# A two-layer encoder trunk: the Hyena filter stored in both parts, its constants and the first products of layer 1 placed anew

## Chip, core and metric

One NeuronCore of a Trainium2 chip runs the whole program. The metric is device time in microseconds (us) of one execution; lower is better.

## What is computed

`x` is 512 tokens by 1024 channels, float32. Layer 0 mixes tokens by latent attention and neighbourhood attention, layer 1 by retention and by a long convolution (Hyena); after each comes a gated feed-forward network with 2816 inner channels. The part that the change is about, cut down:

```python
def hyena_operator(u_proj, short_conv, ..., hy_bias):
    x0, x1, v = jnp.split(dwconv3(u_proj, short_conv), 3, axis=-1)
    h_f, h_b = hyena_filters(L, ...)
    k_circ = jnp.concatenate([h_f, zeros, h_b[1:][::-1]], axis=0)
    u = v * x1
    uf = jnp.fft.rfft(u, n=2 * L, axis=1)
    kf = jnp.fft.rfft(k_circ, n=2 * L, axis=0)
    y = jnp.fft.irfft(uf * kf[None], n=2 * L, axis=1)[:, :L]
    return (y + u * hy_bias) * x0
def bidirectional_retention(rq, rk, rv, rg, decay_fwd, decay_bwd):
    log_f = jax.nn.log_sigmoid(decay_fwd)
    ...
    return rms(o_f + o_b) * jax.nn.silu(rg)
```

## The kernel before

Channels lie on the 128 partitions, tokens in the free dimension. Every float32 matrix is split in two parts, `hi` (rounded to float32r) and `lo` (the remainder), and a product is three matmuls: hi·hi, lo·hi, hi·lo (`mm`, L280 to L282). Weights come in pieces of 128x1024 (`load_weight`, L250): SP loads `raw` (two buffers), ACT casts it to `whi`, DVE subtracts to get `wlo`; there are four buffers of each part, and weights are asked for three ahead. A projection of 128 output channels is 24 matmuls over eight tiles of `h` (`gemm`).

PSUM has eight banks by tag: `pj` two, `A` three, `B` two, `C` one. A product with a tag must wait until an older bank of that tag has been emptied.

A layer's normalization ends in `boundary` (L339). It updates `x`, writes the new `h`, starts the first four projections of the next stage without the token factor (`pre`), and then computes the factor itself: sums of squares by PE (`stats`, L286), the power -1/2 by POOL (`rcol`, L299), four transposes by PE into a `C` bank (`spread`, L316), and ACT's copy to `Rb` (L447). Projections are multiplied by `Rb` when they leave PSUM.

The filter of the long convolution is computed in layer 0's feed-forward stage (`filters`, L963) and stored to DRAM (`filt`) as float32. In layer 1 (`mixer1`, L1061) `dft_consts` loads the transform's constants `dftf` by two DMAs of POOL; `spectrum` (L1008) is a generator: for each of four pairs of parity and trig it loads two tiles `sd` of the filter by ACT's queue, splits them and makes two products `psC` of six matmuls. `mixer1` spills `x` to DRAM (L1065), convolves twelve projections (`conv`, L1072: `v`, then `x1`, then `x0`) with a step of `spectrum` after each of the last eight, transposes `u` (L1101), transforms (`dft`), multiplies spectra on DVE (`pq`, L1140), projects retention's `rv` (`proj_tok`), three `gate`s (L1106), and then makes the inverse transform with `dfti`, four groups of 24 matmuls in `A` banks. `decays` (L1040) computes 8 log decays in 26 small operations of DVE and one of ACT.

A scheduler sets the order on each engine from data dependences, buffer releases and priorities (`high_priority`); `issue_after` keeps an instruction behind a given one. Each engine then runs its queue strictly in order. Lines such as L282 are those of the kernel before; in the queues of the changed kernel shown further down they are that kernel's own, three to a hundred further on.

Of the kernel before, what the change touches and what calls it, by code (L numbers as in the profile page):

```python
# [16 lines left out]
P = 128  # L17
# [188 lines left out]
class Body:  # L206
    def __init__(self, ctx, tc, I, out, dbg=None):
        self.tc, self.nc, self.I, self.out, self.dbg = tc, tc.nc, I, out, dbg
        nc = self.nc
        pool = lambda n, b, **k: ctx.enter_context(tc.tile_pool(name=n, bufs=b, **k))  # L210
        self.cp = pool("cp", 1)
        self.wp = pool("wp", 4)
        self.xp = pool("xp", 8)
        self.hp = pool("hp", 16)
        self.sp = pool("sp", 6)
        self.pp = pool("pp", 8, space=bass.MemoryType.PSUM)
        self.dp = pool("dp", 1, space=bass.MemoryType.DRAM)
# [32 lines left out]
    def load_weight(self, n=1):  # L250
# [88 lines left out]
    def boundary(self, pool, tag, x, prod, gpost, gpre, ns, ftag, perm=False, rin=None):  # L339
# [529 lines left out]
    def ffn(self, p, x, h, pre, l):  # L869
# [18 lines left out]
        for j in range(FT):  # L888
# [5 lines left out]
            nc.vector.tensor_tensor(t, gps, Rb, ALU.mult)  # L894
# [35 lines left out]
    def dft_consts(self, p, name):  # L930
        out = []
        for i, part in enumerate(("hi", "lo")):
            t = p.tile([P, 4, 2, 256], F32R, tag="dft" + part, name=name + part)
            self.nc.gpsimd.dma_start(t.rearrange("p m a b -> p (m a b)"), self.I[name][:, i * 2048:(i + 1) * 2048])
# [28 lines left out]
    def filters(self, new):  # L963
# [28 lines left out]
        for tk in range(4):  # L992
# [10 lines left out]
            for i, src in enumerate((t, n)):  # L1003
                nc.sync.dma_start(self.filt[i, ts], src)
# [3 lines left out]
    def spectrum(self, mats, at, kt, spec):  # L1008
        nc = self.nc
        for par in range(2):  # L1010
            for trig in range(2):
                m = 2 * par + trig
                sd = []
                for hh in range(2):
                    t = self.X("sd", tag="xb")
                    tk = 2 * par + hh
# [3 lines left out]
                for ft in range(2):  # L1020
                    ps = self.PS("C")
                    for hh in range(2):
                        c = slice(ft * P, ft * P + P)
                        self.mm(ps, (mats[0][:, m, hh, c], mats[1][:, m, hh, c]), sd[hh], hh == 0, hh == 1)
                    if par == 0:
                        t = self.X("sp", tag="xb")
                        nc.scalar.activation(t, ps, AF.Copy, scale=1.0 / 512)
                        spec[ft, trig] = t
                    else:
                        e, o, d = spec[ft, trig], kt(), kt()  # L1030
                        nc.vector.scalar_tensor_tensor(o, ps, 1.0 / 512, e, ALU.mult, ALU.add)
                        if trig == 0:
                            nc.vector.scalar_tensor_tensor(d, ps, -1.0 / 512, e, ALU.mult, ALU.add)
                        else:
                            nc.vector.scalar_tensor_tensor(d, ps, 1.0 / 512, e, ALU.mult, ALU.subtract)
                        spec[ft, trig] = (o, d)
                    yield
# [23 lines left out]
    def mixer1(self, p, x, h, pre):  # L1061
        nc = self.nc
        spill = self.dp.tile([D, S], F32, name="xspill")
        for k in range(KT):
            nc.scalar.dma_start(spill[k * P:(k + 1) * P], x[k])  # L1065
        mats = self.dft_consts(p, "dftf")
# [5 lines left out]
        def conv(jj, dst):  # L1072
            ps = pre[jj - 8] if jj >= 8 else self.proj(h, "A" if jj == 4 else "pj")
            t = p.tile([P, S], F32, tag="cv", name=self.nm("cv"))
            nc.vector.tensor_tensor(t, ps, Rb, ALU.mult)
            cw = [self.col(C_SC + i * 12 + jj) for i in range(3)]
            nc.scalar.activation(dst, t, AF.Copy, scale=cw[1])
# [7 lines left out]
        u, x0 = [], [p.tile([P, S], F32, name=f"x0{j}") for j in range(4)]  # L1085
        for j in range(4):
            u.append(conv(8 + j, p.tile([P, S], F32, name=f"u{j}")))
# [84 lines left out]
        lg = self.decays(p)  # L1172
# [124 lines left out]
```

## Time and profile before

| | |
|---|---|
| timed runs | 1308.06, 1312.72, 1312.88 us; median 1312.72 |
| profiled execution | 1307.53 us, its span 1305.8 us |
| busy in the span | PE 97%, weight load 81%, DVE 62%, ACT 45%, POOL 6% |
| granted TensorE clock, mean | 0.993 of full |
| chain that ended last | PE 87%, DVE 5%, ACT 3% |
| retention and Hyena of layer 1 | 668 to 905 us of the span |

The span runs from the first to the last instruction. PE does nearly all that decides the time; what the other engines do matters where PE waits for it. The list of PE's waits and the timelines around them show these places.

### The profile page before, as it was taken

The page shows a single profiled execution, that of the slowest core. Times are in us where ns is not written, and L with a number is a line of the kernel's source. Part 1 is how long each engine was busy: PE and PEld are TensorE (multiplying, and loading weights), DVE is VectorE, ACT ScalarE, POOL GpSimd, SP SyncE. Part 2 cuts the span into 40 slices and gives each one's busy share as a digit, 9 for nine tenths or more (in the row PEclk, how much of TensorE's full clock was granted, in tenths as well). Part 3 has the DMA queues.
Part 4 walks back from the last instruction along what each step waited for, and adds up shares of the span by engine and source line. Part 5 has one row for each costly group of instructions (what it writes and reads, how often), then busy time and mean ns, then how long its engine had stood idle before and what let it go on. Part 6 is the DMA issues. An engine that isn't in the chain of part 4 may idle for free.

```text
span 1305.8 us, 16380 instructions
## 1 busy us (share of the span) xinstructions
PE 1271.7 (97%) x6370; PEld 1057.5 (81%) x6370; DVE 813.9 (62%) x1298; ACT 582.9 (45%) x943; POOL 80.9 (6%) x73
## 2 busy tenths in 40 slices
PE   9999799999999999999999999999999999999997
PEld 7788677997888788888987878778988888888886
DVE  6679898478766665322588785774875555552223
ACT  5456798456533333222454245544653333332221
POOL 4021322000000000000000000000000000000002
PEclk9999899999999999999999989999999999999999
DMA  7222012223434333333264233214233333333331
GB/s 269 86 65 79 3 33 68 82 79 116 121 123 135 122 113 97 99 111 97 83 226 128 58 120 95 81 49 130 66 113 98 97 97 97 97 97 104 107 97 65
DMA packets 41563, 130.62 MB, mean 100 GB/s; under 512 B 4652, under 2 KB 6892, under 8 KB 40973
## 3 DMA queue, kind: packets, MB, share of 16 engines
q1 hardware_dynamic: 35868, 116.92, 29.0%
q10 hardware_dynamic: 5040, 8.45, 2.0%
q0 software_dynamic: 576, 4.19, 0.9%
q8 instruction: 50, 0.82, 0.3%
q14 instruction: 29, 0.23, 0.1%
HBM read 123.26 MB, written 6.29 MB: 99 GB/s over the span
## 4 chain that ended last, share of the span: by engine, by line
PE 87%; DVE 5%; ACT 3%; issue 2%; DMA 1%; POOL 1%; SPq 0%; DVEq 0%; POOLq 0%; ACTq 0%
PE pspj L280 17%; PE pspj L282 17%; PE pspj L281 17%; PE psA L280 10%; PE psA L282 10%; PE psA L281 10%; DVE wlo L260 1%; ACT e L794 1%; DMA raw<-in_w 1%; PE psB L292 1%; PE psB L671 1%; PE psB L810 1%; DVE h L334 1%; ACT whi L259 1%; PE psC L282 1%
## 5 line engine op out<-in xcount | busy, mean ns | idle before, releaser
L259 ACT CAST whi<-raw 128x1024 fp32r<-128x1024 f32 (+1 forms) x200 | 209.1, 1048 | 432.1 <-PE pspj L281 237.8
L260 DVE TENSOR_TENSOR wlo<-raw,whi 128x1024 fp32r<-128x1024 f32 (+1 forms) x200 | 246.6, 1235 | 204.8 <-ACT whi L259 202.8
L280 PE MATMUL pspj<-h,whi 128*128 128x512 f32 (+1 forms) x664 | 250.5, 377 | 2.8 <-DVE v L599 2.7
L281 PE MATMUL pspj<-h,whi 128*128 128x512 f32 (+1 forms) x664 | 249.6, 376 | 0.0
L282 PE MATMUL pspj<-h,wlo 128*128 128x512 f32 (+1 forms) x664 | 249.4, 376 | 0.0
L282 PE MATMUL psA<-h,wlo 128*128 128x512 f32 (+1 forms) x424 | 155.4, 367 | 0.7 <-DVE wlo L260 0.7
L280 PE MATMUL psA<-h,whi 128*128 128x512 f32 (+1 forms) x424 | 156.1, 368 | 0.0
L281 PE MATMUL psA<-h,whi 128*128 128x512 f32 (+1 forms) x424 | 155.1, 366 | 0.0
L280 PEld LDWEIGHTS pspj<-h,whi 128*128 128x128 f32 x664 | 125.5, 189 | 25.4 <-DVE v L599 3.1
L282 PEld LDWEIGHTS pspj<-h,wlo 128*128 128x128 f32 x664 | 125.4, 189 | 22.2
L281 PEld LDWEIGHTS pspj<-h,whi 128*128 128x128 f32 x664 | 125.5, 189 | 22.0
L280 PE MATMUL pspj<-ahi,whi 128*128 128x512 f32 x308 | 121.4, 394 | 0.0
L282 PE MATMUL pspj<-ahi,wlo 128*128 128x512 f32 x308 | 120.7, 392 | 0.0
L281 PE MATMUL pspj<-alo,whi 128*128 128x512 f32 x308 | 119.5, 388 | 0.0
L282 PEld LDWEIGHTS psA<-h,wlo 128*128 128x128 f32 x424 | 79.8, 189 | 15.5 <-DVE wlo L260 1.9
L280 PEld LDWEIGHTS psA<-h,whi 128*128 128x128 f32 x424 | 80.0, 189 | 14.8 <-issue 2.6
L281 PEld LDWEIGHTS psA<-h,whi 128*128 128x128 f32 x424 | 80.0, 189 | 12.4
L894 DVE TENSOR_TENSOR t<-psA,Rb 128x512 f32<-128x512 f32 x40 | 27.6, 691 | 83.4 <-PE psA L282 83.3
L282 PEld LDWEIGHTS pspj<-ahi,wlo 128*128 128x128 f32 x308 | 57.8, 188 | 13.5
L281 PEld LDWEIGHTS pspj<-alo,whi 128*128 128x128 f32 x308 | 57.8, 188 | 12.9
L280 PEld LDWEIGHTS pspj<-ahi,whi 128*128 128x128 f32 x308 | 57.9, 188 | 11.5
L299 POOL TENSOR_TENSOR r<-v,mhalf 128x2 f32<-128x2 f32 (+1 forms) x14 | 13.7, 977 | 847.7 <-DVE v L297 690.2
(360 smaller groups left out, 2140.1 us busy)
## 6 DMA issues: line engine op xcount, KB each, us to landing
raw<-in_w SPq DMA_DIRECT2D x198, 512.0 KB, 3.5
x<-in_xT SPq DMA_DIRECT2D x16, 256.0 KB, 4.8
fflt<-in_fwin SPq DMA_DIRECT2D x8, 256.0 KB, 2.9
xspill<-f ACTq DMA_DIRECT2D x8, 256.0 KB, 2.6
sd<-filt ACTq DMA_DIRECT2D x8, 256.0 KB, 3.3
x<-xspill ACTq DMA_DIRECT2D x8, 256.0 KB, 3.2
rpb<-in_rpb SPq DMA_DIRECT2D x4, 384.0 KB, 4.6
filt<-fs SPq DMA_DIRECT2D x4, 256.0 KB, 2.5
```

What stands on the lines that cost most here:

```text
L259: nc.scalar.copy(hi[:, c], raw[:, c])
L260: nc.vector.tensor_tensor(lo[:, c], raw[:, c], hi[:, c].bitcast(F32), ALU.subtract)
L280: nc.tensor.matmul(ps, stat[0], mov[0], start=start, stop=False)
L281: nc.tensor.matmul(ps, stat[0], mov[1], start=False, stop=False)
L282: self.last_mm = nc.tensor.matmul(ps, stat[1], mov[0], start=False, stop=stop).ins
L292: nc.tensor.matmul(ps[:, j:j + 1], a[:, j * P:(j + 1) * P], self.ones, start=a is accs[0], stop=a is accs[-1])
L299: self.pow = nc.gpsimd.tensor_tensor(r, v, self.mhalf[:, :c], ALU.pow)
L334: self.nc.vector.scalar_tensor_tensor(lo, src, g, hi.bitcast(F32), ALU.mult, ALU.subtract)
L671: tr = lambda o, i: nc.tensor.transpose(o, i, self.ident)
L794: nc.scalar.activation(e, ps, AF.Exp, bias=nmx, accum_out=den[:, i:i + 1])
L810: nc.tensor.transpose(pt[:, i * P:(i + 1) * P], es[i][:, j * P:(j + 1) * P], self.ident)
L894: nc.vector.tensor_tensor(t, gps, Rb, ALU.mult)
```

## The change

**What it does.** `filt` holds both parts of the filter: after each step of `filters` ACT and DVE split the two results and SP stores four tiles instead of two. In layer 1, POOL loads the 16 stored tiles straight into the operands of `spectrum`, right behind the two constants `dftf`, all at high priority; the loads by ACT's queue and the eight splits are gone. The first four projections (`pre`) are scaled into `x0` tiles at once, all four, and convolved from there. The spill of `x` is issued behind the second `u`. `decays` is computed in layer 0's feed-forward stage. A `gate` and `rv` leave PSUM by an ACT copy, and DVE works on the copy in SBUF. A weight's cast by ACT is kept behind the last `Rb` copy (`hold`) if the weight is asked for after it.

```diff
-        self.filt = self.dp.tile([2, S, HC], F32, name="filt")
+        self.filt = self.dp.tile([2, 2, S, HC], F32, name="filt")
+        self.hold = None
...
             with self.tc.high_priority(WP):
-                nc.scalar.copy(hi[:, c], raw[:, c])
+                with self.tc.issue_after(self.hold) if self.hold is not None else ExitStack():
+                    nc.scalar.copy(hi[:, c], raw[:, c])
...
-            nc.scalar.copy(self.Rb, self.spread(self.rcol, "C"))
+            self.hold = nc.scalar.copy(self.Rb, self.spread(self.rcol, "C")).ins
...
-            nc.vector.tensor_tensor(t, gps, Rb, ALU.mult)
+            scaled = nc.vector.tensor_tensor(t, gps, Rb, ALU.mult)
+            if l == 0 and j == 4:
+                with self.tc.issue_after(scaled.ins):
+                    self.decay = self.decays(self.cp)
...
             for i, src in enumerate((t, n)):
-                nc.sync.dma_start(self.filt[i, ts], src)
+                hl = self.X("fh", F32R), self.X("fl", F32R)
+                self.split_to(*hl, src)
+                for part in range(2):
+                    nc.sync.dma_start(self.filt[part, i, ts], hl[part].bitcast(F32))
...
     def spectrum(self, mats, at, kt, spec):
+        for m in range(4):
+            parts.append([at(m % 2) for _ in range(2)])
+            for hh in range(2):
+                tk = 2 * (m // 2) + hh
+                for part in range(2):
+                    with self.tc.high_priority(300), self.tc.issue_after(self.consts):
+                        nc.gpsimd.dma_start(parts[m][hh][part], self.filt[part, m % 2, tk * P:(tk + 1) * P])
+        yield
...
-                    nc.scalar.dma_start(t, self.filt[trig, tk * P:(tk + 1) * P])
-                    sd.append(at(trig))
-                    self.split_to(*sd[-1], t)
...
     def mixer1(self, p, x, h, pre):
-        for k in range(KT):
-            nc.scalar.dma_start(spill[k * P:(k + 1) * P], x[k])
-        mats = self.dft_consts(p, "dftf")
+        x0 = [p.tile([P, S], F32, name=f"x0{j}") for j in range(4)]
+        with self.tc.high_priority(300):
+            mats = self.dft_consts(p, "dftf")
...
+        next(steps)
+
         for j in range(4):
-            u.append(conv(8 + j, p.tile([P, S], F32, name=f"u{j}")))
+            scaled(pre[j], x0[j])
+        u = []
+        for j in range(4):
+            u.append(conv(8 + j, p.tile([P, S], F32, name=f"u{j}"), x0[j]))
+            if j == 1:
+                with self.tc.issue_after(self.taken):
+                    for k in range(KT):
+                        nc.scalar.dma_start(spill[k * P:(k + 1) * P], x[k])
...
         def gate():
-            g, ps = self.X("rg", tag="xb"), self.proj(h)
-            nc.vector.tensor_tensor(g, ps, Rb, ALU.mult)
+            g = self.X("rg", tag="xb")
+            nc.scalar.copy(g, self.proj(h))
+            nc.vector.tensor_tensor(g, g, Rb, ALU.mult)
...
+            t = self.X("rv", tag="xb")
+            nc.scalar.activation(t, ps, AF.Copy, scale=rcol[:, j:j + 1])
             rv.append(two("t1"))
-            self.scaled(rv[-1], ps, rcol[:, j:j + 1], slice(0, S))
+            self.split_to(*rv[-1], t)
...
-        lg = self.decays(p)
+        lg = self.decay
```

**What it moves.** The programs' queues differ only here and in small exchanges in retention. First POOL's queue at the start of layer 1, before and now (`r` and `rcol` are the powers of the boundary, `filt` the stored filter; in brackets the semaphores waited for: DMASW are eight counters that POOL's transfers take in turn).

```order
L299 TENSOR_TENSOR r_5695<-v_5693,mhalf 128x2 [waits DVE_49]
L934 DMA dftfhi<-in_dftf 128x2048 [waits DMAHW2_49,DMAHW1_49,DMAHW5_49,DVE_49,DMAHW6_49,PE_49,Activation_49]
L299 TENSOR_TENSOR rcol_5879<-v_5982,mhalf 128x4 [waits DVE_49]
L934 DMA dftflo<-in_dftf 128x2048 [waits DMAHW6_49]
```

The same stretch of POOL's queue in the changed kernel:

```order
L302 TENSOR_TENSOR r_5767<-v_5765,mhalf 128x2 [waits DVE_49]
L940 DMA dftfhi<-in_dftf 128x2048 [waits PE_49,Activation_49]
L940 DMA dftflo<-in_dftf 128x2048 [waits PE_49]
L1026 DMA t_1107_6076<-filt 128x512 [waits DMAHW5_49]
...
L1026 DMA t_1110_6079<-filt 128x512 [waits DMAHW0_49,DMASW0_49]
...
L1026 DMA t_1118_6095<-filt 128x512 [waits DMAHW4_49,DMASW0_49]
L1026 DMA t_1122_6103<-filt 128x512 [waits DMAHW6_49,DMASW1_49]
L302 TENSOR_TENSOR rcol_5951<-v_6054,mhalf 128x4 [waits DVE_49]
L940 DMA dftihi<-in_dfti 128x2048 [waits DMASW2_49,PE_49]
```

The constants stood around `rcol`, the first behind a product of PE that belongs to the sum of squares. Now both constants and all 16 filter loads stand ahead of `rcol`, and from the seventh filter load on each waits for the transfer eight places before it.

PE's queue at the same place, before and now (`psA` is the fifth projection, `ident,rcol` the transposes for `Rb`, `psC<-t` the first product of the filter, `pspj` the sixth projection).

```order
L282 MATMUL psA_6036<-h_5592,wlo_5713 128x512
L316 MATMUL psC_5985<-ident,rcol_5879 128x128 [waits Pool_49]
L280 MATMUL psA_6036<-h_5594,whi_5712 128x512
...
L282 MATMUL psA_6036<-h_5600,wlo_5713 128x512
L280 MATMUL psC_6085<-t_1101_6075,dftfhi 128x512 [waits DMASW0_49,Activation_49]
L281 MATMUL psC_6085<-t_1102_6076,dftfhi 128x512 [waits DVE_49]
L280 MATMUL pspj_6094<-h_5586,whi_5718 128x512 [waits DVE_49]
L282 MATMUL psC_6085<-t_1101_6075,dftflo 128x512 [waits DMASW1_49]
```

The same place in the changed kernel:

```order
L285 MATMUL psA_6136<-h_5672,wlo_5785 128x512
L319 MATMUL psC_6057<-ident,rcol_5951 128x128 [waits Pool_49]
L283 MATMUL psC_6173<-t_1107_6076,dftfhi 128x512 [waits DMASW2_49,DMASW0_49,Activation_49]
L284 MATMUL psC_6173<-t_1108_6077,dftfhi 128x512 [waits DMASW4_49]
L285 MATMUL psC_6173<-t_1107_6076,dftflo 128x512 [waits DMASW1_49]
...
L284 MATMUL psC_6173<-t_1110_6079,dftfhi 128x512 [waits DMASW0_49]
L285 MATMUL psC_6173<-t_1109_6078,dftflo 128x512
L283 MATMUL pspj_6182<-h_5658,whi_5790 128x512 [waits DVE_49]
```

The transposes moved behind twelve more matmuls of the fifth projection and now stand directly ahead of the filter's product, which uses the same single `psC` bank; the wait for the constants is no longer spread over two places.

PE's queue at the inverse transform, before and now (the first row ends `proj_tok`; `pspj` are gates, `dfti` the inverse transform).

```order
L282 MATMUL psA_6659<-whi_6661,h_5601 128x512
L280 MATMUL psA_6898<-dftihi,t_1206_6550 128x256 [waits DMASW2_49,Activation_49]
L281 MATMUL psA_6898<-dftilo,t_1206_6550 128x256 [waits DMASW3_49]
L282 MATMUL psA_6898<-dftihi,t_1207_6551 128x256 [waits DVE_49]
...
L280 MATMUL psA_6898<-dftihi,t_1241_6648 128x256 [waits Activation_49]
L281 MATMUL psA_6898<-dftilo,t_1241_6648 128x256
L280 MATMUL pspj_6797<-h_5586,whi_6691 128x512 [waits DVE_49]
```

In the changed kernel `proj_tok` is followed by:

```order
L285 MATMUL psA_6711<-whi_6713,h_5673 128x512
L283 MATMUL pspj_6857<-h_5658,whi_6743 128x512 [waits Activation_49]
...
L285 MATMUL pspj_6892<-h_5672,wlo_6774 128x512
L283 MATMUL pspj_6927<-h_5658,whi_6803 128x512 [waits Activation_49]
...
L285 MATMUL pspj_6927<-h_5672,wlo_6804 128x512
L283 MATMUL psA_6961<-dftihi,t_1210_6602 128x256 [waits DMASW2_49]
L284 MATMUL psA_6961<-dftilo,t_1210_6602 128x256 [waits DMASW3_49]
L285 MATMUL psA_6961<-dftihi,t_1211_6603 128x256
```

The first group of the inverse transform stood ahead of the three gates, with a wait for nearly every operand; now it stands behind the gates' 72 matmuls, with the other three groups after it, and the gates wait for ACT where they waited for DVE.

## Rows read from the trace of the kernel before

**Rows 1.** The page's part 1, busy time by engine.
```profile
PE 1271.7 (97%) x6370; PEld 1057.5 (81%) x6370; DVE 813.9 (62%) x1298; ACT 582.9 (45%) x943; POOL 80.9 (6%) x73
```

**Rows 2.** Timeline of PE, layer 1's start: start, us, engine, line, op, [wait].
```profile
669.73 0.48 PE L280 MATMUL psA<-h,whi 128*128 128x512 f32 x1
...
672.98 0.65 PE L316 MATMUL psC<-ident,rcol 128*128 128x128 f32 x4
...
676.01 0.39 PE L282 MATMUL psA<-h,wlo 128*128 128x512 f32 x1
676.93 0.47 PE L280 MATMUL psC<-t,dftfhi 128*128 128x512 f32 x1 [0.53 <-DMA dftfhi<-in_dftf]
677.23 0.39 PE L281 MATMUL psC<-t,dftfhi 128*128 128x512 f32 x1
677.46 0.40 PE L280 MATMUL pspj<-h,whi 128*128 128x512 f32 x1
680.10 0.50 PE L282 MATMUL psC<-t,dftflo 128*128 128x512 f32 x1 [2.24 <-DMA dftflo<-in_dftf]
```

**Rows 3.** Timeline of POOL, 640 to 760 us.
```profile
645.50 1.08 POOL L299 TENSOR_TENSOR r<-v,mhalf 128x2 f32<-128x2 f32 x1 [8.04 <-DVE v L297]
...
671.52 1.40 POOL L299 TENSOR_TENSOR rcol<-v,mhalf 128x4 f32<-128x4 f32 x1 [0.28 <-DVE v L295]
672.89 0.59 POOL L934 DMA_DIRECT2D dftflo<-in_dftf  x1
...
748.52 0.54 POOL L934 DMA_DIRECT2D dftilo<-in_dfti  x1
```

**Rows 4.** Timeline of PE, fourth filter product and first transpose.
```profile
695.73 0.50 PE L280 MATMUL psC<-t,dftfhi 128*128 128x512 f32 x1 [0.69 <-ACT sp L1027]
...
698.64 0.50 PE L1101 MATMUL psB<-ident,u 128*128 128x128 f32 x2 [1.26 <-DVE u L1090]
```

**Rows 5.** Timeline of PE, inverse transform and the gate after it.
```profile
769.45 0.38 PE L280 MATMUL psA<-dftihi,t 128*128 128x256 f32 x1 [1.78 <-ACT t L274]
...
770.61 0.39 PE L282 MATMUL psA<-dftihi,t 128*128 128x256 f32 x1 [0.65 <-DVE t L275]
770.83 0.28 PE L280 MATMUL psA<-dftihi,t 128*128 128x256 f32 x1
770.95 0.28 PE L281 MATMUL psA<-dftilo,t 128*128 128x256 f32 x1
771.81 0.58 PE L282 MATMUL psA<-dftihi,t 128*128 128x256 f32 x1 [0.58 <-DVE t L275]
...
774.54 0.63 PE L280 MATMUL pspj<-h,whi 128*128 128x512 f32 x1
774.97 0.63 PE L281 MATMUL pspj<-h,whi 128*128 128x512 f32 x1
```

**Rows 6.** Stretches: us, busy PE, PEld, DVE, ACT, POOL, clock, DMA, GB/s.
```profile
742.00:766.00 24.00, 24.00 (x108) 19.86 (x107) 23.16 (x38) 7.18 (x10) 1.06 (x2) 1.00 0.32 110
...
772.00:778.00 6.00, 6.00 (x21) 5.23 (x22) 5.87 (x8) 3.06 (x5) 0.00 (x0) 0.50 0.36 96
```

**Rows 7.** DMA issues: queue, op, count, KB, median us to landing.
```profile
dftilo<-in_dfti POOLq DMA_DIRECT2D x1, 1024.0 KB, 7.4
```

**Rows 8.** Timeline of ACT, third weight's cast and the copy of the factor.
```profile
673.82 1.05 ACT L259 CAST whi<-raw 128x1024 fp32r<-128x1024 f32 x1 [0.80 <-DMA raw<-in_w]
674.78 0.57 ACT L447 COPY Rb<-psC 128x512 f32<-128x512 f32 x1
```

**Rows 9.** Tile `raw` (weights as loaded), 640 to 700 us, ten loads.
```profile
DMA to landing us min/median/max: 3.4/3.7/6.8
```

**Rows 10.** Timeline of DVE: a weight remainder, a multiply-add, a scaling.
```profile
687.44 1.23 DVE L260 TENSOR_TENSOR wlo<-raw,whi 128x1024 fp32r<-128x1024 f32 x1 [0.65 <-ACT whi L259]
688.58 0.74 DVE L1078 SCALAR_TENSOR_TENSOR u<-cv,cols,u 128x511 f32<-128x511 f32 x1
...
690.15 0.69 DVE L1075 TENSOR_TENSOR cv<-psA,Rb 128x512 f32<-128x512 f32 x1
```

More of the change, by code (lines that the diff above doesn't have):

```diff
@@ L933, in dft_consts @@
             t = p.tile([P, 4, 2, 256], F32R, tag="dft" + part, name=name + part)
-            self.nc.gpsimd.dma_start(t.rearrange("p m a b -> p (m a b)"), self.I[name][:, i * 2048:(i + 1) * 2048])
+            self.consts = self.nc.gpsimd.dma_start(t.rearrange("p m a b -> p (m a b)"), self.I[name][:, i * 2048:(i + 1) * 2048]).ins
             out.append(t)
@@ L1009, in spectrum @@
         nc = self.nc
[L1010 to L1013, printed above, removed]
-                for hh in range(2):
-                    t = self.X("sd", tag="xb")
-                    tk = 2 * par + hh
-                    nc.scalar.dma_start(t, self.filt[trig, tk * P:(tk + 1) * P])
-                    sd.append(at(trig))
-                    self.split_to(*sd[-1], t)
[L1020 to L1028, printed above, removed]
-                    else:
[L1030 to L1037, printed above, removed]
@@ new lines, in spectrum @@
+        parts = []
+        for m in range(4):
[6 more added lines that the diff above has]
+        yield
+        for m in range(4):
+            par, trig = m // 2, m % 2
+            sd = parts[m]
+            for ft in range(2):
+                ps = self.PS("C")
+                for hh in range(2):
+                    c = slice(ft * P, ft * P + P)
+                    self.mm(ps, (mats[0][:, m, hh, c], mats[1][:, m, hh, c]), sd[hh], hh == 0, hh == 1)
+                if par == 0:
+                    t = self.X("sp", tag="xb")
+                    nc.scalar.activation(t, ps, AF.Copy, scale=1.0 / 512)
+                    spec[ft, trig] = t
+                else:
+                    e, o, d = spec[ft, trig], kt(), kt()
+                    nc.vector.scalar_tensor_tensor(o, ps, 1.0 / 512, e, ALU.mult, ALU.add)
+                    if trig == 0:
+                        nc.vector.scalar_tensor_tensor(d, ps, -1.0 / 512, e, ALU.mult, ALU.add)
+                    else:
+                        nc.vector.scalar_tensor_tensor(d, ps, 1.0 / 512, e, ALU.mult, ALU.subtract)
+                    spec[ft, trig] = (o, d)
+                yield
@@ L1063, in mixer1, with scaled, conv @@
         spill = self.dp.tile([D, S], F32, name="xspill")
-        for k in range(KT):
-            nc.scalar.dma_start(spill[k * P:(k + 1) * P], x[k])
-        mats = self.dft_consts(p, "dftf")
+        x0 = [p.tile([P, S], F32, name=f"x0{j}") for j in range(4)]
+        with self.tc.high_priority(300):
+            mats = self.dft_consts(p, "dftf")
         two = lambda tag: tuple(p.tile([P, S], F32R, tag=tag, bufs=8, name=self.nm(tag)) for _ in range(2))
         rcol, Rb = self.rcol, self.Rb
-        def conv(jj, dst):
-            ps = pre[jj - 8] if jj >= 8 else self.proj(h, "A" if jj == 4 else "pj")
-            t = p.tile([P, S], F32, tag="cv", name=self.nm("cv"))
+        def scaled(ps, t):
             nc.vector.tensor_tensor(t, ps, Rb, ALU.mult)
+            return t
+        def conv(jj, dst, t=None):
+            if t is None:
+                t = scaled(self.proj(h, "A" if jj == 4 else "pj"), p.tile([P, S], F32, tag="cv", name=self.nm("cv")))
             cw = [self.col(C_SC + i * 12 + jj) for i in range(3)]
-            nc.scalar.activation(dst, t, AF.Copy, scale=cw[1])
+            self.taken = nc.scalar.activation(dst, t, AF.Copy, scale=cw[1]).ins
             nc.vector.scalar_tensor_tensor(dst[:, 1:], t[:, :S - 1], cw[0], dst[:, 1:], ALU.mult, ALU.add)
@@ L1084, in mixer1 @@
                               lambda: p.tile([P, S], F32, tag="t2", bufs=8, name=self.nm("ks")), ks)
-        u, x0 = [], [p.tile([P, S], F32, name=f"x0{j}") for j in range(4)]
+        next(steps)
         for j in range(4):
-            u.append(conv(8 + j, p.tile([P, S], F32, name=f"u{j}")))
+            scaled(pre[j], x0[j])
[6 more added lines that the diff above has]
+                        nc.scalar.dma_start(spill[k * P:(k + 1) * P], x[k])
         for j in range(4):
```

## Prediction, made before the changed kernel was run

> **What bounds the kernel now.** I read the page first: TensorE (PE) is busy in 97% of the span, so only the time in which PE stands still, or runs below full clock, can be won [rows 1]. The list of PE's waits came next: between 640 and 780 us, the start of layer 1, lie seven of them, and the feed-forward stages before and after hold almost none. Then PE's instructions in order of time at these places, where the reader should look at start times: at full clock one 512-column product starts 0.23 us after the last, as 677.46 after 677.23 [rows 2].
>
> Three stalls and one slow stretch matter:
> - *The front.* The first filter product waits 0.53 us for `dftfhi`, the third 2.24 us for `dftflo` [rows 2]: POOL issues `dftflo` only after it has computed `rcol` [rows 3].
> - *The fourth filter product and the first transpose* wait 0.69 us for ScalarE's (ACT's) copy out of the only `psC` bank, and 1.26 us for VectorE's (DVE's) first `u` times `x1` [rows 4].
> - *The inverse transform* waits 1.78, 0.65 and 0.58 us for `pq` values [rows 5]. DVE is the engine that is late there: it is busy 23.16 of 24 us [rows 6].
> - *The clock.* After those three gaps the granted clock of 772 to 778 us is 0.50, the lower of the two levels (1.2 GHz) [rows 6]; products start 0.43 us apart [rows 5].
>
> **What each part of the change is worth.** The sum is made against the profiled execution, 1307.53 us (span 1305.8 and 1.7 around it). The three timed runs have a median of 1312.72, 0.4% above it; I carry the gain in us over to that median.
>
> 1. *Constants and filter earlier: the 2.8 us of the front go.* The constants now lie over memory that the last feed-forward products free, and POOL reaches them once it has finished the second `r`, which ended at 646.6 [rows 3]. The first filter product needs them near 676. The filter's 16 quarter-MB transfers follow on POOL. An issue by POOL took 0.54 us [rows 3], so 18 take 10 us, to 657; this is the nearest row, as POOL has never issued this shape. The data: `dftilo`, the second of two MB issued one behind the other, landed 7.4 us after its issue, so the two came at some 265 GB/s [rows 3, 7]. Four MB are all that the last issue waits for (eight counters take turns, so the 18th waits for the 10th): 16 us, to 663. All six MB: 24 us, to 670. `rcol`'s power stands behind them on POOL and starts at 671.5 today; its transposes moved behind 12 more products (2.8 us), so it may start up to 2.8 us later, less hand-offs, at no cost. So this hides, with some 8 us to spare.
> 2. *What takes the front's place: 0.9 us.* The transposes of `rcol` and the first filter product now follow each other directly in the same `psC` bank; 12 products stood between them. ACT must copy the bank out first: 0.57 us [rows 8] and two hand-offs of some 0.16 us, the part of the 0.92 us between 676.01 and 676.93 that is neither wait nor pitch [rows 2]. Lower end 0.6. Upper end: the same copy stands behind the cast of the third weight, which was ready at 674.87, 0.8 us before the transposes would end (24 x 0.23 after 669.73, plus 0.4 for the four transposes, whose 0.65 us overlap with what follows: 675.65) [rows 2, 8]. Its load took the usual 3.4 us; the slowest took 6.8 [rows 9]. If it is slowed that much by the filter's transfers the wait grows by 2.6, to 3.5 us.
> 3. *First products: 1.3 us go.* DVE first empties the four banks, then convolves. Ahead of the first `u` times `x1` it has 5 scalings, 10 shifted multiply-adds and 3 weight remainders, at 0.60, 0.66 and 1.14 us from start to start (rows of 0.69, 0.74 and 1.23, which overlap by 0.09) [rows 10]: 13 us; from 676.4 that is 689.4, and up to 690.6 with waits for ACT. PE gets to the transposes after 66 products from 676.4: 691.6. The spare time is the 26 small operations of `decays` and the eight splits of `sd`, which left this place. ACT's eight spill issues move in between `u1` and `u2`, some 3.3 us; they are covered by DVE's work on `u0` and `u1`.
> 4. *The `psC` copy: 0.1 goes.* Two filter products still follow each other with only two transposes between. I keep 0.6 of the 0.69 us.
> 5. *Products between the transforms leave by ACT, and the inverse transform moves behind three gates: 3.0 us and the slow clock go.* The last `pq` that it waited for came before 771.81 [rows 5], and PE now comes there after 72 products, 16.5 us later. The gates need two `pspj` banks. Before, DVE freed them, behind all its `pq` work; now ACT does, as soon as the products end, and ACT has room (7.18 of 24 us) [rows 6]. The clock: 12 products of 256 columns took 2.73 us (771.81 to 774.54) and would take 1.44 at a pitch of 0.12; eight more lost 0.20 each. That is 1.3 + 1.6 = 2.9 us [rows 5].
> 6. *At nothing:* eight more casts on ACT, eight subtractions on DVE, eight stores on SP and the `decays` with one more table load, all in the first feed-forward stage, where PE is not kept waiting and weights lie three ahead (16 us of products). If that cover went, each of the four filter steps could cost a store's landing, for which a tile of the next block now waits: at most the 7.4 us of the slowest row [rows 7]. The weight casts behind `Rb` keep the copy of part 2 from standing behind two more casts; alone they win nothing.
>
> Each removed gap also takes a restart of about 0.16 us with it, six gaps, 1.0 us. Sum: 2.8 + 1.3 + 0.1 + 3.0 + 2.9 + 1.0 - 0.9 = **10.2 us**. The profiled execution would be 1297.3, the median **1302.5 us**, 0.8% faster. With the ends of part 2, the gain lies between 7.6 and 10.5.
>
> **Rivals.**
> - *POOL becomes the bound; slower.* `rcol`, and with it every product's scale, is behind 18 issues. At p us per issue POOL is free at 646.6 + 18p; from about 673.8 on, each us is lost. p = 1.5 costs nothing, p = 2.1 eats the gain, p = 2.5 is 0.5% slower. At 2.7, five times the row, POOL is free at 695.2, 21.4 us are lost, 11.2 net: 1324. For it: DVE is busy almost without pause in that stretch too, and the shape is new on POOL. Against it: the issue at 748.52 took 0.54 us [rows 3] within a stretch in which DVE was 97% busy [rows 6]. The Trainium skill, SBUF — State Buffer, "SBUF: two separate sides", speaks against this change: descriptors of POOL's transfers are written through a port that DVE locks in some modes, and a transfer of 0.62 us alone took 3.1 there; by that figure the kernel would come out near 1331 (an estimate). But it names copies, casts and `tensor_scalar` for this, and `tensor_tensor` not, and the row at 748.52 agrees with that. Chance 0.06.
> - *The front's wait comes back in another form; no change.* The third weight comes 3.4 us late (2.6 more at the copy), the first `u` stays late (1.3), and its late banks cost a us: gain 5.3, 1307.4. For it: ACT's and DVE's queues are in order, with 3.3 us of new issues in ACT's. Against it: the transfers should be over when that weight is asked for, at 670.2. Chance 0.20.
> - *The move doesn't do what it says at the inverse transform:* ACT's copy of the first gate stands behind casts that wait for DVE's `pq`; if a gate then waits as long as the transform did, the clock falls as well and 6.4 us stay: gain 3.8, 1308.9. Against it: those `pq` were there by 771.81 [rows 5], and that bank is wanted again only 48 products, 11 us, after the transform's old start. Chance 0.10.
>
> **How the numbers follow.** Forecast 0.64 (gains of 7.6 to 10.5 and a little beyond), rivals 0.06, 0.20 and 0.10. About 0.5% (6.6 us) is what a measurement of this kernel can tell from no change; the runs before lie between 1308.06 and 1312.88. Faster by more than that: the forecast and a third of the two middle rivals, where only half of their loss comes, 0.72; same 0.21; slower 0.07. The range takes in both levels of the runs: from 1307.5 less 12 to the third rival with the higher level, 1295 to 1311.
>
> **What would show it.** Right: no wait for `dftf` in PE's list; the two constants issued near 646.6 and `rcol` not later than now against PE's sum of squares; a first wait on `Rb` of about 1 us; the inverse transform without waits, and a clock of 1.00 around it. Wrong: PE waiting for `rcol` (POOL), for the third weight's cast, or for `pspj` banks at the gates; or the same stalls gone with no gain, which would put the loss into the tail of retention, whose steps are interleaved anew.

## The result and the profile after

Four runs of the changed kernel lie between 1295.72 and 1298.06 us, median 1297.43; the kernel before had 1312.1 in the same comparison. The ratio is 0.9892, 95% interval 0.987 to 0.9915: 14 us faster (11 to 17), where 10.2 us and 1302.5 us were forecast, with a range of 1295 to 1311. The two profiled executions differ by less: spans of 1305.8 and 1296.3 us, 9.5 us. Both figures are taken up below.

The page's part 1, beside [rows 1], with PE still the engine that is busy nearly all the time:

```profile
PE 1268.5 (98%) x6370; PEld 1056.6 (82%) x6370; DVE 814.6 (63%) x1298; ACT 587.3 (45%) x951; POOL 90.1 (7%) x89
```

The list of waits of the changed kernel, PE alone, 640 to 920 us (engine, what waits, for whom: total us, times, longest):

```profile
PE psB L319 <- POOL r L302: 2.8, 4, 1.2
PE psA L285 <- DVE wlo L263: 0.7, 1, 0.7
PE psC L283 <- ACT Rb L450: 0.7, 1, 0.7
PE psC L283 <- ACT sp L1038: 0.5, 1, 0.5
```

No wait for `dftf`, for `u` or for `pq` is left. The first two rows were there before, at 2.8 and 0.7 us. The third is the new wait that the forecast put in the front's place. PE's timeline at the front, to set beside [rows 2, 4]:

```profile
677.75 0.60 PE L319 MATMUL psC<-ident,rcol 128*128 128x128 f32 x4
679.02 0.50 PE L283 MATMUL psC<-t,dftfhi 128*128 128x512 f32 x1 [0.68 <-ACT Rb L450]
...
694.23 0.39 PE L1123 MATMUL psB<-ident,u 128*128 128x128 f32 x2
695.08 0.50 PE L283 MATMUL psC<-t,dftfhi 128*128 128x512 f32 x1 [0.46 <-ACT sp L1038]
```

The transposes of `u` start without a wait, for VectorE's (DVE's) `u` times `x1` is through 1.4 us ahead of PE:

```profile
692.15 0.69 DVE L1112 TENSOR_TENSOR u<-u,x 128x512 f32<-128x512 f32 x1
```

ACT's queue, beside [rows 8], has the third weight's cast, done before the transposes start, then the copy, and only then the fourth weight's cast:

```profile
675.98 1.05 ACT L262 CAST whi<-raw 128x1024 fp32r<-128x1024 f32 x1 [3.73 <-DMA raw<-in_w]
678.38 0.58 ACT L450 COPY Rb<-psC 128x512 f32<-128x512 f32 x1 [1.35 <-PE psC L319]
678.86 1.05 ACT L262 CAST whi<-raw 128x1024 fp32r<-128x1024 f32 x1
```

POOL's queue, beside [rows 3]:

```profile
648.89 0.76 POOL L940 DMA_DIRECT2D dftfhi<-in_dftf  x1
649.64 0.54 POOL L940 DMA_DIRECT2D dftflo<-in_dftf  x1
650.17 3.18 POOL L1026 DMA_DIRECT2D t<-filt  x6
655.20 0.53 POOL L1026 DMA_DIRECT2D t<-filt  x1 [1.85 <-DMA dftfhi<-in_dftf]
...
665.11 0.53 POOL L1026 DMA_DIRECT2D t<-filt  x1 [0.91 <-DMA t<-filt]
673.86 1.03 POOL L302 TENSOR_TENSOR rcol<-v,mhalf 128x4 f32<-128x4 f32 x1 [8.22 <-DVE nlg L1207]
```

18 issues (0.76 and 0.54 us for the constants, 0.53 to 0.59 for the filter) with waits between them end at 665.6; POOL then stands idle for 8.2 us until `rcol` can be computed. At the inverse transform, beside [rows 5, 6], PE's timeline and then the stretches of 24 and 6 us (busy PE, PEld, DVE, ACT, POOL; clock, DMA, GB/s):

```profile
780.09 0.39 PE L285 MATMUL pspj<-h,wlo 128*128 128x512 f32 x1
780.32 0.28 PE L283 MATMUL psA<-dftihi,t 128*128 128x256 f32 x1
```
```profile
742.00:766.00 24.00, 24.00 (x107) 19.89 (x106) 23.96 (x39) 9.58 (x15) 1.13 (x2) 1.00 0.31 110
...
772.00:778.00 6.00, 6.00 (x28) 4.99 (x27) 4.95 (x7) 4.37 (x6) 0.00 (x0) 1.00 0.53 172
```

DVE is no less full than it was (23.96 of 24 us, 23.16 before), but PE now runs 72 products of gates ahead of the inverse transform, and the clock of 772 to 778 us is 1.00 where it was 0.50.

**Four marks that cut every trace alike.** PE's rows at the sums of squares for `rcol`, at the transform's first product into a `B` bank, at the inverse transform's last product and at the last product of all; first the kernel before, then the changed one:

```profile
668.92 0.94 PE L292 MATMUL psB<-ones,acc 128*128 128x1 f32 x8
...
738.62 0.43 PE L280 MATMUL psB<-t,dftfhi 128*128 128x512 f32 x1
...
801.17 0.28 PE L282 MATMUL psA<-dftihi,t 128*128 128x256 f32 x1
...
1298.12 0.43 PE L316 MATMUL psB<-ident,r 128*128 128x128 f32 x2 [1.10 <-POOL r L299]
```
```profile
671.26 0.95 PE L295 MATMUL psB<-ones,acc 128*128 128x1 f32 x8
...
735.79 0.43 PE L283 MATMUL psB<-t,dftfhi 128*128 128x512 f32 x1
...
791.71 0.28 PE L285 MATMUL psA<-dftihi,t 128*128 128x256 f32 x1
...
1288.53 0.56 PE L319 MATMUL psB<-ident,r 128*128 128x128 f32 x2 [1.10 <-POOL r L302]
```

Their differences are the stretches A (front and first products, 69.70 us before, 64.53 now), B (transforms, 62.55 and 55.92) and C (retention to the end, 496.95 and 496.82). The changed kernel gains 5.2 + 6.6 + 0.1 = **11.9 us** there. Ahead of the first mark it is 2.3 us later, where nothing was forecast. The same marks in all profiles; the last column measures the slow clock between 640 and 912 us, as the sum over stretches of 4 us of (1 - granted clock) x 4. It is an upper end of what the clock cost, since time in which PE stood still anyway counts too:

| kernel | first mark | A | B | C | slow clock |
|---|---|---|---|---|---|
| before | 668.92 | 69.70 | 62.55 | 496.95 | 3.4 |
| before, second profile | 668.48 | 72.53 | 60.85 | 498.35 | 5.2 |
| changed | 671.26 | 64.53 | 55.92 | 496.82 | 0 |
| e1 gates by DVE | 670.72 | 64.53 | 61.52 | 496.95 | 1.7 |
| e2 gates alone | 671.07 | 71.36 | 55.89 | 496.99 | 1.7 |
| e3 constants late | 670.59 | 64.79 | 55.90 | 496.81 | 0 |
| e5 decays back | 667.93 | 66.40 | 55.90 | 496.29 | 0 |
| e6 float32 filter | 670.73 | 68.94 | 55.90 | 496.75 | 1.6 |
| e7 no hold | 670.59 | 70.46 | 55.91 | 496.77 | 3.4 |
| e8 two issues | 671.05 | 64.56 | 55.88 | 496.84 | 0 |
| e9 two banks | 670.79 | 63.23 | 55.91 | 496.34 | 0 |
| e10 later factor | 671.33 | 64.54 | 55.87 | 494.70 | 0 |
| e11 both | 671.16 | 63.26 | 55.92 | 494.79 | 0 |
| e12 constants alone | 673.60 | 73.52 | 60.80 | 498.39 | 6.8 |

Where the clock does not fall, A and B repeat within 0.1 us from profile to profile (64.53 to 64.56, 55.87 to 55.92), and C, in the kernels that leave retention as it is, within 0.7 (496.29 to 496.99; why it varies more stays open). So A and B show plainly what timed runs leave open.

### The profile page after: what moved, and what is told of

Its sections match the earlier page's. It is cut to its first block, busy times and chain, and to the rows that moved or that the text cites. A ratio compares the mean times of both kernels' runs of the same rounds, so it can differ in the third digit from the quotient of the medians.

```text
span 1296.3 us, 16450 instructions
## 1 busy us (share of the span) xinstructions
PE 1268.5 (98%) x6370; PEld 1056.6 (82%) x6370; DVE 814.6 (63%) x1298; ACT 587.3 (45%) x951; POOL 90.1 (7%) x89
## 4 chain that ended last, share of the span: by engine, by line
PE 90%; ACT 3%; DVE 2%; issue 2%; POOL 1%; DMA 1%; SPq 0%; DVEq 0%; POOLq 0%; ACTq 0%
PE pspj L283 17%; PE pspj L285 17%; PE pspj L284 17%; PE psA L283 11%; PE psA L284 10%; PE psA L285 10%; PE psB L295 1%; ACT e L797 1%; PE psB L674 1%; DVE wlo L263 1%; PE psB L813 1%; PE psC L283 1%; PE psC L284 1%; PE psC L285 1%; DVE h L337 1%
```

## The experiments

In the expectations T is the account by the forecast's terms; the other letters stand for rivals.

**e1 and e2: the gates undone, and the gates alone.**

```diff
# e1, on the changed kernel (rv likewise); e2 is the reverse, on the kernel before
-            g = self.X("rg", tag="xb")
-            nc.scalar.copy(g, self.proj(h))
-            nc.vector.tensor_tensor(g, g, Rb, ALU.mult)
+            g, ps = self.X("rg", tag="xb"), self.proj(h)
+            nc.vector.tensor_tensor(g, ps, Rb, ALU.mult)
```

> The changed kernel with gates and rv leaving PSUM by DVE again, all else kept; the scheduler then puts the first group of the inverse transform ahead of the gates again, as before. The account by terms (T): the waits for pq (3.0 us), the slow clock behind them (2.9) and three restarts (0.5) come back, 6.4 us; against the kernel before a gain of about 4 us by the terms (ratio about 0.997). Rival (F, the front is what counts): with the sd splits and decays gone from DVE's queue upstream, DVE reaches pq earlier, no wait comes back, and the time stays within 1 us of the changed kernel (ratio about 0.990). The trace tells: waits of PE at the inverse transform and the granted clock behind them.

> The kernel before with this part alone: gates and rv leave PSUM by ACT; the scheduler moves the first group of the inverse transform behind three gates. T: the three waits for pq, the slow clock and three restarts go, 6.4 us (ratio about 0.995), and the four stalls of the front and of the first products stay as they were. F: the gates now wait for ACT or the clock falls elsewhere, gain under 2 us (ratio 0.9985 or more).

Measured: e1 1303.2 us, ratio 0.9952 (0.9936 to 0.9968); e2 1304.4 us, 0.9956 (0.9939 to 0.9973); each has a little under half of the gain. (T's ratio for e1 was about 0.997; what the front keeps is more than the 4 us that it gave it.) PE's timeline of e1 shows the three waits at the inverse transform again, in their old sizes:

```profile
766.10 0.38 PE L283 MATMUL psA<-dftihi,t 128*128 128x256 f32 x1 [1.77 <-ACT t L277]
...
767.26 0.38 PE L285 MATMUL psA<-dftihi,t 128*128 128x256 f32 x1 [0.65 <-DVE t L278]
...
768.46 0.39 PE L285 MATMUL psA<-dftihi,t 128*128 128x256 f32 x1 [0.59 <-DVE t L278]
```

Stretch B becomes 61.52 in e1 and 55.89 in e2: this part is worth 5.6 us in the one and 6.7 in the other (4.9 against the second profile of the kernel before), and A and C of e1 are those of the changed kernel. So the rival that the earlier front would supply DVE in time falls. T is right but for 0.8 us in e1: the clock behind the same waits was low for less time there (0.66 and 0.91 in the stretches of 4 us from 768, 1.7 us by the measure of the table; 3.4 in the kernel before).

**e3 and e12: the constants late, and the early constants alone.**

```diff
# e3, on the changed kernel
-        with self.tc.high_priority(300):
-            mats = self.dft_consts(p, "dftf")
+        mats = self.dft_consts(p, "dftf")
-                    with self.tc.high_priority(300), self.tc.issue_after(self.consts):
+                    with self.tc.high_priority(300):
# e12, on the kernel before
-        mats = self.dft_consts(p, "dftf")
+        with self.tc.high_priority(300):
+            mats = self.dft_consts(p, "dftf")
```

> The changed kernel with the two constants dftf asked for without priority: POOL issues the 16 filter loads first, then computes rcol, then issues both constants. The scheduler then puts nine products of the sixth projection and more between filter products. T: the constants are issued near 675 to 676 and land 4 to 7.4 us later, near 680 to 683; PE reaches the third or fifth filter matmul near 681 to 685, so 0 to 3 us of the front's wait come back, and u has the same slack: 0 to 3 us slower than the changed kernel (ratio 0.989 to 0.992 against the kernel before). Rival (P, POOL's issues ahead of rcol cost something): rcol starts no earlier than in the changed kernel and nothing changes at it.

> The kernel before with one part of the change alone: the two constants dftf are asked for at high priority, so POOL issues both ahead of rcol. The transposes for Rb move behind the whole fifth projection, and the filter product directly behind them. The forecast's own sum for this part: 2.8 us of the front's wait go and 0.9 come back, the stretch falls from 69.7 (72.5 in the second profile) to about 67.8. T as it stands now, after the run in which the constants came late at no cost: the two waits for the constants go, but the Rb copy comes 1.3 to 2.5 us later against the sums of squares (5.9 us after their start before, 7.1 in the changed kernel), so DVE's chain to the first u, with its splits and decays still in it, ends later too; PE waits for u what it no longer waits for constants; 70 to 72, no gain.

Measured: e3 1297.51 us, 0.9916 (0.9901 to 0.9932), A 64.79: issued at 674.2 and 674.8 behind `rcol`, the constants were in time, though only just: `dftflo` landed 9.6 us after its issue, at 684.4, and the first product with it starts at 684.5. The scheduler had put nine products of the sixth projection ahead of the first filter product, and more ahead of this one. PE's wait is now that of the nine, for the first scaling out of a `pspj` bank, and no longer for the copy to `Rb`:

```profile
679.07 0.50 PE L283 MATMUL pspj<-h,whi 128*128 128x512 f32 x1 [1.40 <-DVE x L1083]
```

e12 1311.95 us, 1.0025 (1.0009 to 1.004): **slower**. ACT's timeline of e12, and PE's:

```profile
684.03 1.04 ACT L259 CAST whi<-raw 128x1024 fp32r<-128x1024 f32 x1 [4.38 <-DMA raw<-in_w]
684.98 0.58 ACT L447 COPY Rb<-psC 128x512 f32<-128x512 f32 x1
```
```profile
685.61 0.79 PE L280 MATMUL psC<-t,dftfhi 128*128 128x512 f32 x1 [4.92 <-ACT Rb L447]
```

The constants no longer bind; the cast of a fourth weight does. It waits 4.38 us for its raw load, the `Rb` copy is queued behind it, and the filter product waits for the bank. The expectation had the direction, but took the copy to be 1.3 to 2.5 us later against the first mark; it is 5.5 later (11.4 us behind the mark, 5.9 before), the slow clock follows, and A is 73.5, not 70 to 72. By the pitch of PE's rows the clock took some 2.3 us of that; without it A would be 71.2, where the two profiles of the kernel before, reckoned in the same way, have 69.7 and 71.0. So even then the early constants alone win nothing. (The profiled execution of e12, 1315.75 us, was the slowest of its ten, and its first mark, up to which it is the kernel before, came 4.7 us later than in the first profile of that kernel.)

**e4: the kernel before, profiled again**, unchanged.

> The kernel before, unchanged, profiled once more. The gain by the medians of the runs is 14 us, by the two profiled executions 9.5 us. T: the profiled execution was the fastest of the kernel before, and what differs is the stretch up to 650 us that the change does not reach, and in which the two profiled executions already differ by 2.4 us; a second profile shows the same stalls between 650 and 910 us within 0.5 us in all and differs, if at all, ahead of 650 us. Rival (H, a hidden part): in a slower execution the stalls or the slow clock between 650 and 910 us are longer by 3 us or more, and the change removes those too.

Measured: 1309.62 us. Ahead of the first mark it agrees within 0.5 us with the first profile; A + B + C are 2.5 us longer. So T falls and H holds, if at less than its 3 us: the front's waits were longer,

```profile
677.16 0.47 PE L280 MATMUL psC<-t,dftfhi 128*128 128x512 f32 x1 [1.19 <-DMA dftfhi<-in_dftf]
...
680.84 0.52 PE L282 MATMUL psC<-t,dftflo 128*128 128x512 f32 x1 [2.74 <-DMA dftflo<-in_dftf]
```

and the clock fell in two places where it had not (stretches of the second profile):

```profile
680.00:684.00 4.00, 3.16 (x8) 2.56 (x9) 3.50 (x8) 2.32 (x4) 0.00 (x0) 0.65 0.42 121
772.00:776.00 4.00, 2.87 (x13) 2.36 (x14) 4.00 (x7) 2.91 (x5) 0.00 (x0) 0.67 0.32 123
844.00:848.00 4.00, 2.74 (x10) 2.21 (x10) 2.07 (x4) 0.95 (x2) 1.26 (x1) 0.63 0.36 131
```

In the first profile, 680 to 684 and 844 to 848 us had a clock of 1.00.

**e5, e6 and e7: three parts undone, one each.**

```diff
# e5
-        lg = self.decay
+        lg = self.decays(p)
# e6: filters stores src as before, POOL loads 8 float32 tiles at the same place, and
-            sd = parts[m]
+            sd = [at(trig) for _ in range(2)]
+            for hh in range(2):
+                self.split_to(*sd[hh], parts[m][hh])
# e7
-                with self.tc.issue_after(self.hold) if self.hold is not None else ExitStack():
-                    nc.scalar.copy(hi[:, c], raw[:, c])
+                nc.scalar.copy(hi[:, c], raw[:, c])
```

> The changed kernel with decays computed in layer 1 again. Of its 26 small operations DVE now takes 11 in an idle stretch ahead of the third weight's remainder and 15 between that remainder and the first scaling. T: 15 dependent ones at some 0.2 us from start to start are 3 us behind 678.3, so the first scaling starts near 681.3 and not at 679.0, 2.3 us later; PE wants that pspj bank at 680.5, so it waits about 1.5 to 2 us more there; the stretch from the sums of squares to the transform (64.53 us in the changed kernel, 69.70 in the kernel before) becomes 66 to 66.5. Rival (F, the constants and loads alone did it): no wait, 64.5.

> The changed kernel with the filter stored as one float32 part, as before: POOL loads eight tiles at the same early place and ACT and DVE split them in layer 1. Seven casts of ACT now stand ahead of the copy to Rb and seven subtractions of DVE ahead of the first scaling. T: 7 x 0.57 us on ACT put the Rb copy near 681 to 682 (678.38 in the changed kernel), 7 x 0.6 on DVE the first scaling near 683 (679.0); PE waits for both, 3 to 4 us more; the stretch becomes 67.5 to 68.5 and the ratio to the kernel before 0.993 to 0.995. Rival (F): splits fit in where ACT and DVE wait anyway (4 us of idle each ahead of the third weight), 64.5 to 65.

> The changed kernel without the rule that keeps later weight casts behind the Rb copy: ACT's queue then has the casts of the fourth and fifth weight ahead of that copy. T: the fifth weight's raw buffer comes free when DVE has made the third remainder, 678.3; load 3.4 us, cast 1.0, so the copy starts near 682.9 and not at 678.4, and PE, which needs the psC bank, waits 4.5 us more, DVE's first scaling starts 5 us later: the stretch becomes 69 to 69.5, ratio 0.994 to 0.996. Rival: ACT has room and the raw loads are early; under 1 us, 64.5 to 65.5.

Measured: e5 1298.03 us, 0.9892 (0.9865 to 0.9919), A 66.40 as T said, with this row of PE:

```profile
678.91 0.50 PE L283 MATMUL pspj<-h,whi 128*128 128x512 f32 x1 [1.57 <-DVE x L1081]
```

(Its timed runs alone, with an interval of 0.5%, would not have shown it.) e6 1302.99 us, 0.9928 (0.9905 to 0.9951), A 68.94, 0.4 us over T's range with a slow clock behind the wait. ACT's rows of e6:

```profile
676.84 3.73 ACT L277 CAST t<-sd 128x512 fp32r<-128x512 f32 x7
680.48 0.57 ACT L450 COPY Rb<-psC 128x512 f32<-128x512 f32 x1
```

e7 1301.97 us, 0.9919 (0.9895 to 0.9942), A 70.46. ACT, then PE:

```profile
681.19 1.04 ACT L261 CAST whi<-raw 128x1024 fp32r<-128x1024 f32 x1 [2.95 <-DMA raw<-in_w]
682.14 0.58 ACT L449 COPY Rb<-psC 128x512 f32<-128x512 f32 x1
```
```profile
682.77 0.79 PE L282 MATMUL psC<-t,dftfhi 128*128 128x512 f32 x1 [5.11 <-ACT Rb L449]
```

The mechanism and the place of the copy are T's (the first mark is 0.7 us earlier in e7, so is the copy); the slow clock behind the gap comes on top (0.57 and 0.58 in the two stretches from 680, some 2.1 us by the pitch of PE's rows, as part of it passed while PE waited), and the 0.46 us of wait for `sp` goes. In A the three parts are worth 1.9, 4.4 and 5.9 us, together more than the 5.2 us that A gained: they don't add up, because each keeps something out of the way of the one copy to `Rb` and the scalings behind it. The early place of the filter loads, the four scalings at once and the later spill were not undone singly; what they are worth stays open.

**e8: twice the issues on POOL.**

```diff
-                        nc.gpsimd.dma_start(parts[m][hh][part], self.filt[part, m % 2, tk * P:(tk + 1) * P])
+                        for c in (slice(0, 256), slice(256, 512)):
+                            nc.gpsimd.dma_start(parts[m][hh][part][:, c], self.filt[part, m % 2, tk * P:(tk + 1) * P, c])
```

> The changed kernel with each of the 16 filter loads issued as two halves, so that POOL issues 34 transfers ahead of rcol and not 18, for the same bytes. T: an issue takes 0.53 us whatever it carries; 34 take 18 us from 648.9, and the waits for earlier transfers end when the data has come; POOL is through near 667 to 671, rcol starts at 673.9 as now, and the time stays within 1 us (stretch 64.5 to 65.5). Rival (P, POOL becomes the bound): issues get dearer while DVE is busy; at 1 us each POOL is through at 683, rcol 9 us late, stretch 73 and ratio about 0.998.

Measured: 1298.25 us, 0.9891 (0.9869 to 0.9913), A 64.56. POOL's last rows:

```profile
664.00 7.92 POOL L1027 DMA_DIRECT2D t<-filt  x15 [0.40 <-DMA t<-filt]
673.65 1.03 POOL L302 TENSOR_TENSOR rcol<-v,mhalf 128x4 f32<-128x4 f32 x1 [1.72 <-DVE nlg L1208]
```

15 issues took 7.92 us, 0.53 each. All 34 end at 671.9 (667 to 671 expected), 1.7 us before `rcol` can start. P falls: twice as many issues cost nothing, and the 8.2 us to spare were real.

**e9, e10 and e11: what is left.**

```diff
# e9 (spread keeps its last transpose as self.last_tr)
-                ps = self.PS("C")
+                ps = self.PS("B" if m < 2 and ft == 0 else "C")
...
-                    self.mm(ps, (mats[0][:, m, hh, c], mats[1][:, m, hh, c]), sd[hh], hh == 0, hh == 1)
+                    with self.tc.issue_after(self.last_tr):
+                        self.mm(ps, (mats[0][:, m, hh, c], mats[1][:, m, hh, c]), sd[hh], hh == 0, hh == 1)
# e10, in r2
             r = self.stats([sq], P)
             yield
+            yield
```

> The changed kernel with two of the filter's first four products in a B bank and not in the single C bank: the first one, kept behind the transposes for Rb, and the third. T: the waits for the Rb copy (0.68 us and its restart, 1.15 in all) and for the sp copy (0.79 in all) go; behind the first product PE now takes a projection, and its pspj bank is emptied by DVE's first scaling about 0.4 us after PE gets there. The stretch from the sums of squares to the transform falls from 64.5 to 63.0 to 63.4; about 0.1% of the time. Rival: the first u becomes the limit, which had some 1.4 us to spare; 64 to 64.5.

> The changed kernel with the last step of a retention head one step of the interleaving later, so that other products stand between the sums of squares of a head and the transposes of its factor; the scheduler moves this for the first two of four heads. T: the two waits for POOL's power there (0.66 and 1.38 us with their restarts) go, the other two stay; the stretch from the end of the inverse transform to the last factor falls from 91.9 to 89.7 to 90.0, 2.0 us in all (0.16%). Rival: the later head output is waited for by the output projection, no gain.

> The changed kernel with both of these, two banks and the later factor. T: the two gains lie in different stretches and add up, 3.2 to 3.6 us, some 1294 us by the level of the changed kernel's runs; ratio to the kernel before about 0.989 less 0.0026. Rival: one is given back, 2 us or less.

Measured: e9 1295.53 us, 0.9894 (0.9877 to 0.9911), A 63.23; e10 1296.18 us, 0.9899 (0.9875 to 0.9924); e11 **1292.81 us, 0.9877 (0.9857 to 0.9897)**. PE's front in e9 has no wait left; the filter's product follows the transposes at once:

```profile
677.28 0.60 PE L319 MATMUL psC<-ident,rcol 128*128 128x128 f32 x4
677.63 0.48 PE L283 MATMUL psB<-t,dftfhi 128*128 128x512 f32 x1
```

In e10 the two waits are gone and C falls by 2.1 us, as much as T said. The stretch that T named, up to the last factor, fell by 0.6 only (91.9 to 91.3): seven more products (409 matmuls there, 402 in the changed kernel) now stand ahead of that factor, 1.6 us that are saved behind it. In e11 A and C are those of e9 and e10 (63.26 and 494.79): the gains add up, 3.3 us. The timed runs do not show this: by the ratios e9 and e10 are level with the changed kernel's 0.9892, and the interval of e11 overlaps with its interval. The stretches alone carry it.

## Why the prediction was right, point by point

- *Front and POOL (parts 1 and 2).* Right in each row: issues at 0.53 us, through at 665.6 (663 was worked out for the data; everything there is 2.3 us later), `rcol` not delayed (2.60 us after the first mark, as before), 8.2 us to spare (some 8 forecast); the new wait on `Rb` 0.68 us, 0.92 with its hand-offs (1.27 from the transposes to the first product, 0.35 in e9), where 0.9 was forecast. Wrong in the credit: the text put the 2.8 us down to the constants' earlier issue. e3 makes them late at no cost, and e12 has them early alone and loses 0.25%. What wins, by e5, e6 and e7, is that ACT has nothing but the `Rb` copy to do when `rcol` comes, and DVE nothing but the scalings behind it.
- *First products (part 3).* The end of `u` times `x1` was forecast at 689.4 to 690.6, PE's arrival at 691.6. Taking off the 2.34 us by which the first mark is later, they came at 690.5 and 691.9.
- *The `psC` copy (part 4).* 0.46 us stayed of 0.69 (0.6 forecast).
- *Inverse transform and clock (part 5).* All three waits, 3.0 us, went, and the gates wait for nothing. The slow clock was sized at 2.9 us from one execution, and luck has a part in that: by the measure of the table it was 3.4 us in this execution, and 1.7 behind the same waits in e1, e4 and e12.
- *At nothing (part 6).* What was moved into the first feed-forward stage costs nothing that can be seen: from 240 to 640 us PE is busy 399.50 of 400 us (399.47 before). The 2.3 us ahead of the first mark arise before that stage, as PE's rows at the transposes of layer 0's own `rcol` show, before and changed:

```profile
293.50 0.65 PE L316 MATMUL psC<-ident,rcol 128*128 128x128 f32 x4 [0.41 <-POOL rcol L299]
...
295.84 0.65 PE L319 MATMUL psC<-ident,rcol 128*128 128x128 f32 x4 [0.42 <-POOL rcol L302]
```

From there to the first mark it is 375.42 us in both. Nor are they the change's: e2 and e12, which are the kernel before up to the first mark, have them too (671.1 and 673.6), and e5, which is the changed kernel up to the feed-forward stage, does not. The clock was 0.57 in 36 to 40 us in the changed kernel, and 1.00 in both profiles of the kernel before; the rest stays open. "Alone they win nothing" of the weight casts stands untested, since no run has them alone; but the part deserved a price: without it, the others lose 5.9 us in A (e7).
- *The sum.* 11.9 us between the marks against 10.2. Waits that went, less new ones: (0.53 + 2.24 + 0.69 + 1.26) - (0.68 + 0.46) = 3.6 in A, where 2.8 + 1.3 + 0.1 - 0.9 = 3.3 were forecast, and 3.0 in B as forecast. The clock gave back 2.9, as forecast, by the pitch of PE's rows (the 3.4 of the table includes time in which PE stood still), C 0.1, and 2.3 are left for restarts, net of those at the two waits that stay, where 1.0 was forecast. That is the most mis-sized term: a gap delays its second product by another 0.1 us, and the transposes of `rcol` amid a projection cost 0.3 ahead of them and 0.1 behind, which the change removed.
- *Profile and median.* The profiled execution of the kernel before was faster than each run timed beside it, and that of the changed kernel, 1298.06 us, was the slowest of its four. The runs of the kernel before scatter from 1306.4 to 1315.6 in all comparisons, those of the changed kernel from 1295.7 to 1298.1: e4 shows one cause, longer waits at the constants and a clock that falls behind them in one execution and not in another. The change removes those places, so it should gain more in the median than from that profile. Not every us of the 14 is shown: the medians of the kernel before in the later comparisons were 1309.0 to 1312.0, which makes the gain 11.6 to 14.5. And the range was 16 us wide: that the time fell into it says less for the account than the rows do.
- *The chances.* A third of the two middle rivals is 0.10, so the chance of a gain of more than 0.5% comes out at 0.74 and not at 0.72.
- *The rivals.* POOL as the bound: the 16 loads took POOL 527 to 585 ns each while DVE was busy 27.3 of 28 us (640 to 668), and the 32 of e8 527 to 655. The Trainium skill, SBUF — State Buffer, "SBUF: two separate sides", says that copies, casts and `tensor_scalar` of DVE can hold up such transfers, and that `tensor_tensor` was not seen to. The trace agrees with the second half: from 640 to 668 us DVE ran `tensor_tensor` and `scalar_tensor_tensor` alone. No run here tests the first. The third weight's cast ended at 677.03, ahead of the transposes, so the front's wait did not come back in that form; and the gates did not wait for ACT.

## What to carry to other kernels

When a chain has one narrow place (here a factor that every later product's scaling needs, copied by an in-order engine out of a single bank), parts of a change that clear it are worth little one by one and can even lose: early constants alone made the kernel 0.25% slower. Ask of each part what the next engine in line then has queued ahead. And cut traces at marks that both kernels have: here stretches repeat within 0.1 us where timed runs scatter by several.

## What the runs showed of the hardware

The granted clock fell, or not, behind the same waits. The two waits at the constants (0.5 and 2.2 us) left it at 1.00 in the first profile of the kernel before; in e2, where they were 0.62 and 2.25, it went to 0.83 and 0.75 in the 4-us stretches from 680. The wait of 1.26 us in retention was followed by 0.63 in the second profile and by 1.00 in the first. (A mean between 0.5 and 1 is a mix of the two levels, 1.2 and 2.4 GHz.) By the measure of the table each fall was 1.7 us, or about twice that; what it cost was less where part of it passed in a wait. So a gap in PE is worth more than its length, by an amount that one profile does not tell.

The filter's loads came faster than the forecast's 265 GB/s: from 652 to 668 us POOL's queue alone moved 5.84 MB, 365 GB/s (with the weights' loads, 350 to 434 GB/s in each us). Each of the 16 loads landed 5.1 to 9.9 us after its issue, and the weights loaded in 640 to 700 us took no longer than before (3.3, 3.8 and 6.8 us least, median and most, beside [rows 9]).
